# Experts in order of load: four to a step for the twelve lightest, two to a step for the rest

## The chip, the cores and the metric

One core of one Trainium2 chip runs the whole program in one launch. The metric is device time in microseconds (us) of that core. The kernel before takes 1086.76 us, the median of three runs (1086.59 to 1087.28).

## The reference

Two residual layers on 512 tokens of width 1024. Each has a token mixer (layer 0: gated MLP, layer 1: latent attention) with cross-attention beside it, and ends with a mixture of 32 experts: every token picks one of 4 groups and in it the top 2 of 8 experts.

```
combine = sum(one_hot(expert_id, 32) * weights, axis=1)
gate = einsum('td,edf->tef', x, w_gate)      # per expert: 1024 x 256
up   = einsum('td,edf->tef', x, w_up)        # 1024 x 256
act  = silu(gate) * up * combine
y    = einsum('tef,efd->td', act, w_down)    # 256 x 1024
```

All is float32. An expert's three matrices are 3.15 MB, a layer's experts 100.7 MB. 512 tokens with 2 experts each are 1024 places, 32 per expert on average.

## The kernel before, in words

The experts' stage is `moe` (L982). Every expert has 64 slots (`CAP`), so two experts fill the 128 rows of a step, and a layer has 16 steps; step i works on experts 2i and 2i+1. A step gathers its rows from DRAM by token index (`gather`, L989, on the queue of GpSimd), transposes and scales them (`turn`, L998), multiplies by gate and up (`gate_up`, L1008: for each of 8 slices of the inner width one matmul of 512 columns for each of the two experts, each on its own 64 columns of the array), applies silu and the product, transposes (`act_T`, L1024), multiplies by down (`down`, L1033) and adds the rows of the step before into the tokens (`combine`, L1055: 16 matmuls with a 0/1 matrix, split in a high and a low part). TensorE's order is the program order. So is SyncE's, which issues the weight loads, and GpSimd's; VectorE and ScalarE are ordered by the scheduler of the program.

Weights land in a ring of 39 units of 512 KB (`unit`, L76; `NU`, L50). An expert takes six: four with a quarter of gate and up each, two with half the columns of down (`xload`, L244). The rows of every load in DRAM are 2 KB long, and a gate/up unit is filled by two loads of 256 KB. Six experts (`P = NU // 6`, L1569) are loaded before the stage, while the output projection of the mixer runs (`ahead` and `rest`, L1605 and L1609); the other 26 are queued by `nxt` (L1616) after each step, and each load waits on the chip until the unit's old tenant has been read. A load also waits on one of eight semaphores that the loads use in turn.

Ahead of the stage the router gives each token its experts and a slot in each (`choose`, `place`), `count` (L898) finds the fullest expert, and `mark` (L906) and `fill` (L943) build the token lists of four steps at a time with 0/1 matrices of 512 slots. At the end of the program a branch (L1659) runs a slow dense version (`dense_moe`) if any expert had more than 64 tokens. After layer 0 the same ring takes the weights of layer 1's mixer (`soon`, L1638).

Of the kernel before, what the change touches and what calls it, by code (L numbers as in the profile page):

```python
# [9 lines left out]
F32 = mybir.dt.float32  # L10
# [36 lines left out]
class Kern:  # L47
# [194 lines left out]


    def xload(self, layer, e, parts=range(6)):  # L244
        a, eng = self.a, self.nc.sync
        gu = [steps(a[name][layer, e]) for name in ("moe_w_gate", "moe_w_up")]
        d = a["moe_w_down"][layer, e].rearrange("(p j) f -> p j f", j=2)
        tiles = []
        for p in parts:
            w = self.unit([2, 512] if p > 3 else [2, 2, 256], F32, f"x{layer}_{e}")  # L250
            if p > 3:
                eng.dma_start(w, d[:, :, (p - 4) * 512:(p - 4) * 512 + 512])
            else:
                for u in range(2):
                    eng.dma_start(w[:, u], gu[u][:, p // 2, p % 2 * 2:p % 2 * 2 + 2])
            tiles.append(w)
        return tiles

# [472 lines left out]

NE = 32


def moe_constants(K):
# [12 lines left out]

    K.vals = K.const([NT, 2, 8], BF, "vals")
    col = K.const([1], I32, "col")  # L750
    nc.gpsimd.iota(col, pattern=[[0, 1]], base=0, channel_multiplier=1)
    for t in range(NT):
        nc.vector.memset(K.vals[:, t, :, 0:1], float(128 * t - 1024))
        nc.vector.tensor_copy(K.vals[:, t, :, 1:2], col.unsqueeze(1).to_broadcast([128, 2, 1]))
    K.br = [K.const([36], F32, "br") for _ in range(2)]
# [19 lines left out]
class Route:  # L775
# [4 lines left out]
    def __init__(self, K, layer, keep=False):  # L780
        self.K, self.i, self.keep = K, layer, keep
        self.hT, self.lg, self.of, self.o = ([None] * NT for _ in range(4))
        s = lambda shape, name, dt=F32: K.s(shape, dt, tag=name, bufs=1)
        self.r, self.e, self.slot = s([NT], "rr"), s([NT, 2], "re"), s([NT, 2], "rs")
        self.wr = s([NT, 2, 2], "rw")
        self.oh, self.osum = K.t([NT, 2, 32], BF, "oh", 1), K.t([NT, 32], BF, "os", 1)

# [107 lines left out]
        v.scalar_tensor_tensor(out=self.slot[:, S_], in0=self.e[:, S_], scalar=float(CAP), in1=pos, op0=ALU.mult,  # L895
                               op1=ALU.add)

    def count(self):  # L898

        K, nc = self.K, self.K.nc  # L900
        b = K.bank([32])
        for t in range(NT):
            nc.tensor.matmul(b, K.ones, self.osum[:, t], start=t == 0, stop=t == 3)
        nc.vector.reduce_max(K.over[self.i], b, axis=AX.X)

    def mark(self, g, t):  # L906
# [22 lines left out]
    def carry(self, t):  # L929

        K = self.K
        if t == 0:
            self.c0 = K.bank([4, 8])
            self.b0 = [K.bank([512]) for _ in range(2)]
        for n in range(2):
            K.nc.tensor.matmul(self.b0[n], self.of[t], K.x[t][:, n * 512:n * 512 + 512], start=t == 0, stop=t == NT - 1)
        if t == NT - 1:
            self.x0 = K.k4([D], F32, "xg")
            K.nc.vector.tensor_copy(self.x0[:, 0:512], self.b0[0])
            K.nc.scalar.copy(self.x0[:, 512:1024], self.b0[1])  # L940
        self.fill(self.c0, t, self.o[t])

    def fill(self, c, t, o):  # L943

        K = self.K
        for j in range(2):
            for q in range(4):
                K.last_mm = K.nc.tensor.matmul(c[:, q], o[:, j, ts128(q)], K.vals[:, t, j],  # L948
                                               start=(t, j, q) == (0, 0, 0), stop=(t, j) == (3, 1),
                                               skip_group_check=True)  # L950

    def slots(self, c):

        K, nc = self.K, self.K.nc
        v = nc.vector
        tok, wr, idx = K.s([4], tag="tok", bufs=2), K.s([4, 2], tag="wsl", bufs=2), K.s([4], I32, tag="idx", bufs=2)
        iv = K.s([4, 8], tag="iv", bufs=1)
        v.tensor_reduce(tok, c[:, :, 0:2], axis=AX.X, op=ALU.add)
        v.tensor_scalar(idx, tok, 1024.0, 0.0, op0=ALU.add, op1=ALU.max)
        v.tensor_copy(iv, c)  # L960
        v.tensor_add(wr, iv[:, :, 2:4], iv[:, :, 4:6])
        v.tensor_add(wr, wr, iv[:, :, 6:8])
        v.tensor_mul(wr[:, :, 0], wr[:, :, 0], wr[:, :, 1])
        return tok, wr, idx
# [17 lines left out]
def moe(K, layer, R, X, nxt, on_rows, soon):  # L982
# [4 lines left out]
    groups, xg = {0: R.g0}, {0: R.x0}  # L987

    def gather(i):  # L989
        g, c = divmod(i, 4)  # L990
# [7 lines left out]
    def turn(i):  # L998
# [6 lines left out]
                nc.scalar.mul(xT[:, k], b[:, k % 4], K.gain(2 + layer, k))  # L1005
        return xT

    def gate_up(i, xT, between={}):  # L1008
        b = K.bank([2, 256])
        for k in range(8):  # L1010
            if k in between:
                between[k]()
            for h in range(2):
                nc.tensor.matmul(b[h * 64:h * 64 + 64], xT[:, k, h * 64:h * 64 + 64], X[2 * i + h][k // 2][:, :, k % 2],  # L1014
                                 start=k == 0, stop=k == 7, skip_group_check=True)
        s = K.k1([256], F32, "silu")
        g, c = divmod(i, 4)
# [15 lines left out]
    def down(i, aT):  # L1033
        bs = [K.bank([512]) for _ in range(2)]
        for n in range(2):
            for j in range(2):
                for h in range(2):
                    w = X[2 * i + h][4 + n][:, j]
                    nc.tensor.matmul(bs[n][h * 64:h * 64 + 64], aT[:, j, h * 64:h * 64 + 64], w,  # L1039
                                     start=j == 0, stop=j == 1, skip_group_check=True)  # L1040
# [3 lines left out]
        g, c = divmod(i, 4)  # L1044
# [42 lines left out]
    combine(y, range(NT))  # L1087
    y = down(1, aT)
    gather(3)
    for e in range(4):  # L1090
        nxt(e)
    for i in range(2, 16):
        g, part = i // 4 + 1, i % 4
        fills = R.group(g, part) if g < 4 and part < 2 else None
        last = i == 15
        a = gate_up(i, xT, {MID[t]: lambda t=t: combine(y, [t]) for t in range(2)} if last else {})
        if fills is not None:
            fills()
# [6 lines left out]
        else:  # L1105
            combine(old, range(NT))
            aT = act_T(a)
        if i + 1 < 16:
# [4 lines left out]
        if i + 2 < 16:  # L1113
            gather(i + 2)
        for h in range(2):
            if (i, h) == (12, 1):
                soon(0)
            nxt(2 * i + h)
        if i in (12, 14):
            soon(i // 2 - 5)  # L1120
    begin(3, 1)
    combine(y, [0, 1], None, on_rows)
    combine(y, [2, 3], begun, on_rows)
# [381 lines left out]
def dense_moe(K, layer, R, on_rows):  # L1505
# [1 line left out]
    nc, a = K.nc, K.a  # L1507
    v = nc.vector
    cd = K.dram.tile([NE, S], F32, name=K.nm("comb"))
    hT, r = R.hT, [K.s([1], tag=f"dr{t}", bufs=1) for t in range(NT)]  # L1510
    for t in range(NT):
        v.tensor_copy(r[t], R.r[:, t:t + 1])
# [53 lines left out]
def build(tc, ctx, args, out):  # L1566
# [35 lines left out]
    def sparse(layer, phase, on_last, soon=lambda part: None):  # L1602
# [13 lines left out]
        def nxt(e):  # L1616

            e += P
            if e < NE:
                e0 = e - e % 2  # L1620
                for part in range(4) if e == e0 else (4, 5):
                    for z in (e0, e0 + 1):
                        X[z] = X.get(z, []) + K.xload(layer, z, [part])
        moe(K, layer, R, X, nxt, on_last, soon)

    def dense(layer, phase, on_last):
        with manual():
# [65 lines left out]
```

## Time and profile before

| what | value |
|---|---|
| median of 3 runs | 1086.76 us |
| the profiled execution, its own time | 1085.28 us |
| span of the profile | 1083.2 us |
| TensorE busy, share of the span | 97% |
| granted TensorE clock, mean | 0.997 |
| bytes moved | 262.83 MB |

The span begins with the first recorded instruction and ends with the last; the 2.1 us between it and the execution's time lie outside. A busy TensorE in this profile includes matmuls whose ends are modelled. "PEld" is the load of a matmul's stationary operand, "SPq" the instruction queue of SyncE. A DMA share of 1.0 means that all 16 DMA engines have a packet in hand all the time.

### The profile page before, as it was taken

To read this page: it belongs to the slowest core of one execution; us is meant where nothing else is said; L and a number is where in the kernel's file an instruction comes from. 1 tells how busy PE (TensorE), PEld (TensorE's weight loads), DVE (VectorE), ACT (ScalarE), POOL (GpSimd) and SP (SyncE) were. 2 spreads that over 40 slices of the span, in tenths; PEclk is the share of its full clock that TensorE was granted. 3 is DMA by queue.
4 is the path that set the end of the run, shared out by engine and by line. 5 is a ranking of instruction groups with operands and counts; after the bars stand their busy time and mean duration, and the time that the engine had idled before them with its cause. 6 is when DMAs were issued, how large, how long until landed. Compare 5 with 4: busy or idle time off the path is not lost. (4 is left out here: it accounts for less than half of the span.)

```text
span 1083.2 us, 16471 instructions
## 1 busy us (share of the span) xinstructions
PE 1055.4 (97%) x5548; PEld 710.3 (66%) x5548; DVE 576.5 (53%) x1358; ACT 449.9 (42%) x1220; POOL 204.9 (19%) x423
## 2 busy tenths in 40 slices
PE   8999999999999999999999999989999999999996
PEld 6878888886455455444888888868884544554453
DVE  5644686216444455344767677776043544554443
ACT  6846744123321232222747776765032312322230
POOL 3440200014010111110322663410032101111100
PEclk9999999999999999999999999999999999999999
DMA  9432433886999999997022111124968999999972
GB/s 359 129 120 62 136 113 121 301 320 220 373 383 385 380 387 376 386 386 268 25 52 78 50 27 59 59 67 154 377 227 301 384 385 385 380 383 386 379 263 81
DMA packets 135840, 262.83 MB, mean 243 GB/s; under 512 B 14843, under 2 KB 18143, under 8 KB 135748
## 3 DMA queue, kind: packets, MB, share of 16 engines
q1 hardware_dynamic: 129024, 247.12, 63.9%
q0 software_dynamic: 6720, 14.57, 4.0%
q8 instruction: 47, 0.77, 0.3%
q14 instruction: 45, 0.37, 0.1%
q10 hardware_dynamic: 4, 0.00, 0.0%
HBM read 262.17 MB, written 7.34 MB: 249 GB/s over the span
## 5 line engine op out<-in xcount | busy, mean ns | idle before, releaser
L1014 PE MATMUL ps<-x,xT 128*64 128x512 f32 x1024 | 226.9, 593 | 0.1
L1061 DVE TENSOR_TENSOR x<-x,ps 128x512 f32<-128x512 f32 x248 | 153.4, 682 | 120.1 <-PE ps L1053 120.1
L1014 PEld LDWEIGHTS ps<-x,xT 128*64 128x64 f32 x1024 | 75.5, 137 | 140.3 <-issue 137.0
L1039 PE MATMUL ps<-x,actT 128*64 128x512 f32 x512 | 116.8, 598 | 0.0
L1052 PE MATMUL ps<-yh,cm 128*128 128x512 f32 x256 | 103.9, 406 | 0.0
L1053 PE MATMUL ps<-yl,cm 128*128 128x512 f32 x256 | 100.7, 393 | 0.1
L992 POOL MEMSET xg<- 128x1024 f32 x30 | 28.6, 954 | 365.8 <-PE ps L128 321.9
L1019 ACT ACTIVATE silu<-ps,wsl 128x256 f32<-128x256 f32 x32 | 15.2, 476 | 194.9 <-PE ps L1014 194.9
L132 DVE TENSOR_TENSOR yl<-ps,yh 128x512 fp32r<-128x512 f32 x64 | 44.3, 692 | 68.3 <-ACT yh L131 43.0
L116 PE MATMUL ps<-wh,c 128*128 128x512 f32 x192 | 76.5, 398 | 0.0
L118 PE MATMUL ps<-wh,c 128*128 128x512 f32 x192 | 75.0, 390 | 0.0
L117 PE MATMUL ps<-wl,c 128*128 128x512 f32 x192 | 74.8, 389 | 0.0
L1039 PEld LDWEIGHTS ps<-x,actT 128*64 128x64 f32 x512 | 34.1, 136 | 60.7 <-issue 56.1
L1005 ACT ACTIVATE xT<-ps,G 128x128 f32<-128x128 f32 x256 | 69.7, 383 | 6.8 <-PE ps L128 6.5
L1052 PEld LDWEIGHTS ps<-yh,cm 128*128 128x128 f32 x256 | 48.1, 188 | 29.8 <-issue 21.1
L116 PE MATMUL ps<-wh,hh 128*128 128x512 f32 (+1 forms) x160 | 60.9, 381 | 2.2 <-ACT pm L454 1.1
L219 DVE SCALAR_TENSOR_TENSOR wl<-wr,G,wh 128x512 fp32r<-128x512 f32 (+1 forms) x80 | 55.2, 732 | 10.5 <-ACT wh L209 10.2
L131 ACT CAST yh<-ps 128x512 fp32r<-128x512 f32 x64 | 37.5, 586 | 54.3 <-PE ps L1039 53.8
L118 PE MATMUL ps<-wh,hl 128*128 128x512 f32 (+1 forms) x160 | 59.8, 374 | 0.0
L117 PE MATMUL ps<-wl,hh 128*128 128x512 f32 (+1 forms) x160 | 59.8, 373 | 0.0
L144 ACT ACTIVATE junk<-x 128x512 bf16<-128x512 f32 x32 | 20.2, 631 | 90.1 <-DVE x L610 87.4
L1030 ACT COPY actT<-ps 128x256 f32<-128x256 f32 x32 | 11.9, 373 | 107.4 <-PE ps L128 107.4
(350 smaller groups left out, 2041.7 us busy)
## 6 DMA issues: line engine op xcount, KB each, us to landing
x<-in_moe_w_gate_dram SPq DMA_DIRECT2D x256, 256.0 KB
x<-in_moe_w_up_dram SPq DMA_DIRECT2D x256, 256.0 KB
x<-in_moe_w_down_dram SPq DMA_DIRECT2D x128, 512.0 KB
wr<-in_a_w_in_dram SPq DMA_DIRECT2D x20, 512.0 KB
wr<-in_a_w_out_dram SPq DMA_DIRECT2D x12, 512.0 KB
wr<-in_b_w_out_dram SPq DMA_DIRECT2D x12, 512.0 KB
wr<-in_w_mem_kv_dram SPq DMA_DIRECT2D x8, 512.0 KB
wr<-in_b_w_in_dram SPq DMA_DIRECT2D x8, 512.0 KB
```

Of the source, the lines that this page charges most:

```text
L116: mm(out, A[0], B[0], start=first, stop=False)
L117: mm(out, A[0], B[1], start=False, stop=False)
L118: self.last_mm = mm(out, A[1], B[0], start=False, stop=last)
L131: self.gate(self.nc.scalar.copy(hi, src), after)
L132: return self.nc.vector.tensor_sub(lo, src, hi.bitcast(F32))
L219: b = self.nc.vector.scalar_tensor_tensor(out=l, in0=r, scalar=g, in1=h.bitcast(F32), op0=ALU.mult, op1=ALU.subtract)
L1005: nc.scalar.mul(xT[:, k], b[:, k % 4], K.gain(2 + layer, k))
L1014: nc.tensor.matmul(b[h * 64:h * 64 + 64], xT[:, k, h * 64:h * 64 + 64], X[2 * i + h][k // 2][:, :, k % 2], start=k == 0, stop=k == 7, skip ...
L1039: nc.tensor.matmul(bs[n][h * 64:h * 64 + 64], aT[:, j, h * 64:h * 64 + 64], w, start=j == 0, stop=j == 1, skip_group_check=True)
L1052: nc.tensor.matmul(b, cm[:, ts128(t)], yh[:, sl], start=first, stop=False)
L1053: K.last_mm = nc.tensor.matmul(b, cm[:, ts128(t)], yl[:, sl], start=False, stop=last)
L1061: v.tensor_add(K.x[t][:, sl], K.x[t][:, sl], b)
```

## The change

Experts 0 to 5 keep their place: three steps of two, loaded ahead. The other 26 are ranked on the chip by their token count. The 12 with the fewest tokens get 32 slots each and go four to a step (three steps), the other 14 go in pairs of 64 (seven steps): 13 steps in place of 16. `rank` takes the place of `count`; it computes the rank of each expert, the slot shift of its tokens and the list of expert numbers, and the dense branch is also taken when one of the twelve has more than 32 tokens. SyncE reads the expert numbers of a step into registers, two or four, ahead of that step's first load, and the loads take their DRAM address from the register. Each unit now holds one kind of weight, is filled by one load of 512 KB, and its DRAM rows are 4 KB. Because gate and up are in separate units, `gate_up` runs one matmul of 256 columns for gate and one for up. The groups of `mark` and `fill` cover 3, 4, 4 and 2 steps.

```diff
 def xload(self, layer, e, parts=range(6)):
+        gu = [a[name][layer, ds(e, 1)].rearrange("o (a p j) f -> p a (o j) f", a=2, j=4)
+              for name in ("moe_w_gate", "moe_w_up")]
+        d = a["moe_w_down"][layer, ds(e, 1)].rearrange("o (p j) f -> p (o j) f", j=2)
...
+            w = self.unit([1024] if p > 3 else [4, 256], F32, "xw")
+            eng.dma_start(w, d[:, p - 4] if p > 3 else gu[p % 2][:, p // 2])
...
+FIXED, LIGHT = 6, 12
+SORTED = NE - FIXED
+WIDTH = [2] * (FIXED // 2) + [4] * (LIGHT // 4) + [2] * ((SORTED - LIGHT) // 2)
+GROUPS = ((0, 3), (3, 4), (7, 4), (11, STEPS - 11))
...
-    def count(self):
+    def rank(self):
         b = K.bank([32])
         for t in range(NT):
             nc.tensor.matmul(b, K.ones, self.osum[:, t], start=t == 0, stop=t == 3)
-        nc.vector.reduce_max(K.over[self.i], b, axis=AX.X)
+        v.scalar_tensor_tensor(out=key, in0=b[:, FIXED:NE], scalar=float(NE), in1=mine, ...)
+        v.tensor_tensor(out=less, in0=key.unsqueeze(2).to_broadcast([128, n, n]),
+                        in1=key.unsqueeze(1).to_broadcast([128, n, n]), op=ALU.is_gt)
+        v.tensor_reduce(r, less, axis=AX.X, op=ALU.add)
+        v.scalar_tensor_tensor(out=je, in0=r, scalar=K.col, in1=mine, ..., accum_out=e)
+        K.tr(eb, e[0:n])
...
+        v.tensor_copy(self.ids, eb)
...
+    def expert(self, r):
+        return self.K.nc.values_load(self.ids[0:1, r:r + 1], engines=[ENG.SP], min_val=FIXED, max_val=NE - 1)
...
+    def tiles_of(i):
+        w = 128 // WIDTH[i]
+        return [(slice(h * w, h * w + w), {"tile_position": (0, h * w)} if w == 32 else {}) for h in range(WIDTH[i])]
 def gate_up(i, xT, between={}):
-            for h in range(2):
-                nc.tensor.matmul(b[h * 64:h * 64 + 64], xT[:, k, h * 64:h * 64 + 64], X[2 * i + h][k // 2][:, :, k % 2], ...)
+            for u in range(2):
+                for h, (c, tp) in enumerate(tiles_of(i)):
+                    nc.tensor.matmul(b[c, u], xT[:, k, c], X[i][h][k // 4 * 2 + u][:, k % 4], ..., **tp)
 def down(i, aT):
-                for h in range(2):
-                    w = X[2 * i + h][4 + n][:, j]
+                for h, (c, tp) in enumerate(tiles_of(i)):
+                    nc.tensor.matmul(bs[n][c], aT[:, j, c], X[i][h][4 + j][:, n * 512:n * 512 + 512], ..., **tp)
...
-        R.count()
+        R.rank()
+            for i in range(P // 2, STEPS):
+                ids = [R.expert(rank + h) for h in range(WIDTH[i])]
+                for part in range(6):
+                    for h, e in enumerate(ids):
+                        W[i][h] += K.xload(layer, e, [part])
+        def nxt(i):
+            free = 6 * sum(WIDTH[:i + 1])
+            while state["units"] < free and next(stream, stream) is not stream:
+                pass
```

`PhaseC` (the list of layer 1's mixer weights) is made ahead of the last step's down loads, and its first splits come after step 11 (of 0 to 12) instead of step 14 (of 0 to 15): in both one step ahead of the last.

## Rows read from the trace of the kernel before

**Rows 1.** The page: busy time by engine, and the rows by 40 slices of 27.1 us (TensorE's busy tenths, its granted clock, the DMA engines' busy tenths, GB/s).

```profile
PE 1055.4 (97%) x5548; PEld 710.3 (66%) x5548; DVE 576.5 (53%) x1358; ACT 449.9 (42%) x1220; POOL 204.9 (19%) x423
...
PE   8999999999999999999999999989999999999996
...
PEclk9999999999999999999999999999999999999999
DMA  9432433886999999997022111124968999999972
GB/s 359 129 120 62 136 113 121 301 320 220 373 383 385 380 387 376 386 386 268 25 52 78 50 27 59 59 67 154 377 227 301 384 385 385 380 383 386 379 263 81
```

**Rows 2.** TensorE's instructions in order of time (start us, duration us, line): the first matmuls of the experts' stage in layer 1; the last step of layer 0 and of layer 1, from inside gate and up to the first scatter after down.

```profile
822.73 0.69 PE L1014 MATMUL ps<-x,xT 128*64 128x512 f32 x2
...
501.87 1.46 PE L1014 MATMUL ps<-x,xT 128*64 128x512 f32 x6
...
504.38 2.80 PE L1014 MATMUL ps<-x,xT 128*64 128x512 f32 x12
...
509.25 3.65 PE L1039 MATMUL ps<-x,actT 128*64 128x512 f32 x16
512.83 0.50 PE L1052 MATMUL ps<-yh,cm 128*128 128x512 f32 x1
...
1066.50 3.65 PE L1039 MATMUL ps<-x,actT 128*64 128x512 f32 x16
1070.08 0.50 PE L1052 MATMUL ps<-yh,cm 128*128 128x512 f32 x1
```

**Rows 3.** Busy time of each engine in stretches: start:end and length in us, busy us and instructions of PE, PEld, DVE, ACT, POOL, then granted clock, DMA share, GB/s. From 10 to 15 us most bytes come in rows of 4 KB (the input x), in the other stretches in rows of 2 KB.

```profile
10.00:12.50 2.50, 2.32 (x8) 1.69 (x7) 2.50 (x7) 2.50 (x7) 0.00 (x0) 0.72 1.05 411
12.50:15.00 2.50, 2.50 (x8) 1.93 (x8) 1.70 (x3) 2.50 (x7) 1.38 (x3) 0.60 1.02 406
15.00:20.00 5.00, 5.00 (x24) 4.14 (x23) 2.58 (x4) 3.22 (x7) 2.13 (x6) 1.00 1.05 390
205.00:230.00 25.00, 25.00 (x112) 20.69 (x111) 0.93 (x2) 0.73 (x2) 0.00 (x0) 1.00 1.05 387
285.00:480.00 195.00, 195.00 (x1004) 98.52 (x1004) 98.20 (x191) 53.07 (x153) 24.65 (x26) 1.00 1.05 384
842.00:1040.00 198.00, 198.00 (x1018) 99.45 (x1016) 99.15 (x192) 54.57 (x156) 25.50 (x26) 1.00 1.05 383
```

**Rows 4.** SyncE's queue in order of time (start us, us, line): the loads around the start of the stage in layer 0, the last expert loads (down) and the first loads after them.

```profile
259.14 0.33 SPq L255 DMA_DIRECT2D x<-in_moe_w_up_dram  x1
267.44 0.33 SPq L255 DMA_DIRECT2D x<-in_moe_w_gate_dram  x1
...
480.83 2.57 SPq L252 DMA_DIRECT2D x<-in_moe_w_down_dram  x4
483.53 7.25 SPq L189 DMA_DIRECT2D wr<-in_b_w_in_dram  x7
491.58 0.47 SPq L420 DMA_DIRECT2D kT<-kT_d  x1
```

**Rows 5.** The longest waits of SyncE's queue over the whole program (line that waits, what for, us in total, times, longest us).

```profile
SPq L255 <- DMA x<-in_moe_w_down_dram: 112.9, 111, 1.8
...
SPq L255 <- DMA x<-in_moe_w_up_dram: 42.6, 117, 2.7
SPq L255 <- DMA x<-in_moe_w_gate_dram: 38.7, 119, 1.0
...
SPq L255 <- PE ps L1014: 25.0, 29, 8.2
```

**Rows 6.** The DMA queues in 285 to 480 us (packets, MB, share of 16 engines): SyncE's weight loads, and the gathers on GpSimd's queue.

```profile
q1 hardware_dynamic: 38551, 71.48, 99.9%
q0 software_dynamic: 1728, 3.15, 4.4%
```

**Rows 7.** The page's costliest groups, two of TensorE (line, operation, out<-in, rows*columns of the array, size, count | busy us, mean ns of one | idle before).

```profile
L1014 PE MATMUL ps<-x,xT 128*64 128x512 f32 x1024 | 226.9, 593 | 0.1
L1039 PE MATMUL ps<-x,actT 128*64 128x512 f32 x512 | 116.8, 598 | 0.0
```

**Rows 8.** TensorE in order of time: a gate and up of a step on two column halves, two of its operand loads, and four matmuls on all 128 columns.

```profile
341.21 7.04 PE L1014 MATMUL ps<-x,xT 128*64 128x512 f32 x32
...
341.64 0.14 PEld L1014 LDWEIGHTS ps<-x,xT 128*64 128x64 f32 x2 [0.29 <-issue]
342.07 0.14 PEld L1014 LDWEIGHTS ps<-x,xT 128*64 128x64 f32 x2 [0.28 <-issue]
...
819.38 1.98 PE L936 MATMUL ps<-x,of 128*128 128x512 f32 x4 [0.35 <-DVE of L923]
```

**Rows 9.** All engines in order of time at the start of layer 0's stage, where `count` stands.

```profile
264.16 0.25 PE L903 MATMUL ps<-os,ones 128*128 128x32 bf16 x4
...
264.26 1.29 PE L128 MATMUL ps<-ident,xg 128*128 128x128 f32 x8
264.33 0.17 DVE L958 TENSOR_REDUCE tok<-ps 128x4 f32<-128x8 f32 x1 [0.34 <-PE ps L948]
...
264.61 0.18 DVE L904 TENSOR_REDUCE over<-ps 128x1 f32<-128x32 f32 x1
...
265.39 0.16 DVE L963 TENSOR_TENSOR wsl<-wsl 128x4 f32<-128x4 f32 x1
...
265.47 0.69 PE L1014 MATMUL ps<-x,xT 128*64 128x512 f32 x2
```

**Rows 10.** VectorE's groups by size, for the new instructions of `rank` (columns as in rows 7).

```profile
L1061 DVE TENSOR_TENSOR x<-x,ps 128x512 f32<-128x512 f32 x248 | 153.4, 682 | 120.1 <-PE ps L1053 120.1
...
L450 DVE TENSOR_REDUCE s4dt.float<-ps 128x2 f32<-128x512 f32 x16 | 10.8, 682 | 7.3 <-PE ps L118 7.2
...
L1191 DVE TENSOR_TENSOR ra<-ps,tab 128x128 f32<-128x128 f32 (+1 forms) x20 | 5.5, 275 | 5.0 <-ACT qrow L1370 4.8
```

**Rows 11.** SyncE's queue by line (duration ns: min/median/max; first and last start us): reading one value into a register at L1658, with its two checks; the eight stores of the result.

```profile
L1658 SPq TENSOR_LOAD <-ovi x1: 728/728/728, 1041.8 to 1041.8; - x1
L1658 SPq FUSED_REGOPS  x1: 186/186/186, 1042.6 to 1042.6; - x1
L1658 SPq SEQ_ASSERT  x1: 37/37/37, 1042.8 to 1042.8; - x1
...
L1574 SPq DMA_DIRECT2D out_dram<-x x8: 333/392/986, 1072.1 to 1076.7; - x8
```

More of the change, by code (lines that the diff above doesn't have):

```diff
@@ L245, in xload @@
         a, eng = self.a, self.nc.sync
-        gu = [steps(a[name][layer, e]) for name in ("moe_w_gate", "moe_w_up")]
-        d = a["moe_w_down"][layer, e].rearrange("(p j) f -> p j f", j=2)
+        gu = [a[name][layer, ds(e, 1)].rearrange("o (a p j) f -> p a (o j) f", a=2, j=4)
+              for name in ("moe_w_gate", "moe_w_up")]
+        d = a["moe_w_down"][layer, ds(e, 1)].rearrange("o (p j) f -> p (o j) f", j=2)
         tiles = []
         for p in parts:
[L250 to L255, printed above, removed]
+            w = self.unit([1024] if p > 3 else [4, 256], F32, "xw")
+            eng.dma_start(w, d[:, p - 4] if p > 3 else gu[p % 2][:, p // 2])
             tiles.append(w)
@@ L732, with place_of @@
 NE = 32
+FIXED, LIGHT = 6, 12
+SORTED = NE - FIXED
+WIDTH = [2] * (FIXED // 2) + [4] * (LIGHT // 4) + [2] * ((SORTED - LIGHT) // 2)
+STEPS = len(WIDTH)
+GROUPS = ((0, 3), (3, 4), (7, 4), (11, STEPS - 11))
+def place_of(i):
+    return next((g, i - c) for g, (c, n) in enumerate(GROUPS) if i < c + n)
 def moe_constants(K):
@@ L754, in moe_constants @@
         nc.vector.tensor_copy(K.vals[:, t, :, 1:2], col.unsqueeze(1).to_broadcast([128, 2, 1]))
+    K.col = K.const([1], F32, "colf")
+    nc.vector.tensor_copy(K.col, col)
     K.br = [K.const([36], F32, "br") for _ in range(2)]
@@ L896, in place @@
                                op1=ALU.add)
-    def count(self):
+    def rank(self):
         K, nc = self.K, self.K.nc
+        v = nc.vector
+        n = SORTED
         b = K.bank([32])
@@ L903, in count @@
             nc.tensor.matmul(b, K.ones, self.osum[:, t], start=t == 0, stop=t == 3)
-        nc.vector.reduce_max(K.over[self.i], b, axis=AX.X)
+        z = K.k1([8, 32], F32, "rank")
+        key, r, m, d, je = (z[:, i, 0:n] for i in range(5))
+        e, w, move = z[:, 5, 0:1], z[:, 5, 2:4], z[:, 6, 0:2 * NT]
+        less = K.k2([n, n], BF, "less")
+        mine = K.iota16[:, FIXED:NE]
+        v.scalar_tensor_tensor(out=key, in0=b[:, FIXED:NE], scalar=float(NE), in1=mine, op0=ALU.mult, op1=ALU.add)
@@ new lines, in rank @@
+        v.tensor_tensor(out=less, in0=key.unsqueeze(2).to_broadcast([128, n, n]),
+                        in1=key.unsqueeze(1).to_broadcast([128, n, n]), op=ALU.is_gt)
+        v.tensor_reduce(r, less, axis=AX.X, op=ALU.add)
+        v.scalar_tensor_tensor(out=je, in0=r, scalar=K.col, in1=mine, op0=ALU.is_equal, op1=ALU.mult,
+                               accum_out=e)
+        eb = K.bank([n], p=1)
+        K.tr(eb, e[0:n])
+        v.tensor_scalar(m, r, 2.0, -float(LIGHT), op0=ALU.mult, op1=ALU.add)
@@ new lines, in rank @@
+        v.tensor_max(m, m, r)
+        v.scalar_tensor_tensor(out=d, in0=K.iota16[:, 0:n], scalar=-2.0, in1=m, op0=ALU.mult, op1=ALU.add)
+        by = K.k2([2 * NT, n], F32, "by")
+        v.tensor_tensor(out=by, in0=self.oh.rearrange("p t j e -> p (t j) e")[:, :, FIXED:NE],
+                        in1=d.unsqueeze(1).to_broadcast([128, 2 * NT, n]), op=ALU.mult)
+        v.tensor_reduce(move, by, axis=AX.X, op=ALU.add)
+        v.scalar_tensor_tensor(out=flat(self.slot2), in0=move, scalar=CAP / 2.0, in1=flat(self.slot), op0=ALU.mult,
+                               op1=ALU.add)
@@ new lines, in rank @@
+        self.ids = K.s([n], I32, tag="k_ids", bufs=1, p=1)
+        v.tensor_copy(self.ids, eb)
+        v.tensor_scalar(m, r, float(LIGHT), CAP / 2.0, op0=ALU.is_lt, op1=ALU.mult)
+        v.tensor_add(m, m, b[:, FIXED:NE])
+        v.reduce_max(w[:, 0:1], m, axis=AX.X)
+        v.reduce_max(w[:, 1:2], b[:, 0:FIXED], axis=AX.X)
+        v.tensor_max(K.over[self.i], w[:, 0:1], w[:, 1:2])
+    def expert(self, r):
+        return self.K.nc.values_load(self.ids[0:1, r:r + 1], engines=[ENG.SP], min_val=FIXED, max_val=NE - 1)
@@ L946, in fill @@
         for j in range(2):
-            for q in range(4):
+            for q in range(c.shape[1]):
                 K.last_mm = K.nc.tensor.matmul(c[:, q], o[:, j, ts128(q)], K.vals[:, t, j],
@@ L955, in slots @@
         v = nc.vector
-        tok, wr, idx = K.s([4], tag="tok", bufs=2), K.s([4, 2], tag="wsl", bufs=2), K.s([4], I32, tag="idx", bufs=2)
-        iv = K.s([4, 8], tag="iv", bufs=1)
+        n = c.shape[1]
+        tok, wr, idx = (K.s(shape, dt, tag=tag, bufs=2)[:, 0:n]
+                        for shape, dt, tag in (([4], F32, "tok"), ([4, 2], F32, "wsl"), ([4], I32, "idx")))
+        iv = K.s([32], tag="pj", bufs=1).rearrange("p (q v) -> p q v", q=4)[:, 0:n]
         v.tensor_reduce(tok, c[:, :, 0:2], axis=AX.X, op=ALU.add)
@@ L1012, in gate_up @@
                 between[k]()
-            for h in range(2):
-                nc.tensor.matmul(b[h * 64:h * 64 + 64], xT[:, k, h * 64:h * 64 + 64], X[2 * i + h][k // 2][:, :, k % 2],
-                                 start=k == 0, stop=k == 7, skip_group_check=True)
+            for u in range(2):
+                for h, (c, tp) in enumerate(tiles_of(i)):
+                    nc.tensor.matmul(b[c, u], xT[:, k, c], X[i][h][k // 4 * 2 + u][:, k % 4], start=k == 0 and u == 0,
+                                     stop=k == 7, skip_group_check=True, **tp)
         s = K.k1([256], F32, "silu")
-        g, c = divmod(i, 4)
+        g, c = place_of(i)
         wr = groups[g][1][:, c]
@@ L1036, in down @@
             for j in range(2):
-                for h in range(2):
-                    w = X[2 * i + h][4 + n][:, j]
-                    nc.tensor.matmul(bs[n][h * 64:h * 64 + 64], aT[:, j, h * 64:h * 64 + 64], w,
-                                     start=j == 0, stop=j == 1, skip_group_check=True)
+                for h, (c, tp) in enumerate(tiles_of(i)):
+                    nc.tensor.matmul(bs[n][c], aT[:, j, c], X[i][h][4 + j][:, n * 512:n * 512 + 512],
+                                     start=j == 0, stop=j == 1, skip_group_check=True, **tp)
         yh, yl = K.k4([1024], FR, "yh"), K.k4([1024], FR, "yl")
@@ L1089, in moe @@
     gather(3)
[L1090 to L1095, printed above, removed]
+    nxt(1)
+    for i in range(2, STEPS):
+        g, part = next(((g, i - c + 4) for g, (c, n) in enumerate(GROUPS) if g > 1 and 0 <= i - c + 4 < 2), (0, 0))
+        fills = R.group(g, part) if g else None
+        last = i == STEPS - 1
         a = gate_up(i, xT, {MID[t]: lambda t=t: combine(y, [t]) for t in range(2)} if last else {})
@@ L1112, in moe @@
             groups[g] = R.slots(R.c)
-        if i + 2 < 16:
+        if i + 2 < STEPS:
             gather(i + 2)
[L1115 to L1120, printed above, removed]
+        nxt(i)
+        if i == STEPS - 2:
+            soon(2)
     begin(3, 1)
@@ L1509, in dense_moe @@
     cd = K.dram.tile([NE, S], F32, name=K.nm("comb"))
-    hT, r = R.hT, [K.s([1], tag=f"dr{t}", bufs=1) for t in range(NT)]
-    for t in range(NT):
-        v.tensor_copy(r[t], R.r[:, t:t + 1])
+    rd = K.s([NT], tag="dr", bufs=1)
+    hT, r = R.hT, [rd[:, t:t + 1] for t in range(NT)]
+    v.tensor_copy(rd, R.r)
     with K.tc.manual_schedule(engines={ENG.PE}):
@@ L1613, in sparse, with loads @@
         nc.scalar.activation(K.s([1]), R.ex[:, 0:1], AF.Silu)
-        R.count()
[L1616 to L1624, printed above, removed]
+        R.rank()
+        W = {i: [X[2 * i], X[2 * i + 1]] for i in range(P // 2)}
+        state = {"units": 0}
+        def loads():
+            rank = 0
+            for i in range(P // 2, STEPS):
+                ids = [R.expert(rank + h) for h in range(WIDTH[i])]
+                rank += WIDTH[i]
+                W[i] = [[] for _ in ids]
+                for part in range(6):
+                    if (i, part) == (STEPS - 1, 4):
+                        soon(0)
+                    for h, e in enumerate(ids):
+                        W[i][h] += K.xload(layer, e, [part])
+                        state["units"] += 1
+                        yield
+        stream = loads()
+        def nxt(i):
+            free = 6 * sum(WIDTH[:i + 1])
+            while state["units"] < free and next(stream, stream) is not stream:
+                pass
+        moe(K, layer, R, W, nxt, on_last, soon)
     def dense(layer, phase, on_last):
```

17 lines of the change are left out of this document (10 added, 7 removed).

## The prediction

> **What bounds the kernel now.** I read the page first. TensorE is busy in 97% of the span and its granted clock is at full speed; but in the two stretches where the experts run (the 11th to 18th slice and the 32nd to 38th) the DMA engines are also busy all the time, at 373 to 387 GB/s [rows 1]. So the stage has two candidates, and the order of time decides. The first matmul of layer 0's stage starts at 265.47 [rows 9], the last down ends at 509.25 + 3.65 = 512.9 [rows 2]: 247.4 us for 16 steps, 15.46 each. In layer 1 it is 822.73 to 1066.50 + 3.65 = 1070.15, again 247.4. The last expert load has landed by 491.6: the load of kT issued then is the eighth after it, and a load waits for the eighth before it [rows 4]. That is 18 us before down of the last step begins. So TensorE sets the end, with the transfers a step ahead of it. That the transfers are not far behind shows in SyncE's waits: mostly for an earlier load, seldom for TensorE to free a unit [rows 5]. One step's weights, 6.29 MB at 384 GB/s, take 16.4 us, more than the 15.46 of TensorE; the six experts loaded ahead are what keeps TensorE from waiting.
>
> The reader is to keep both budgets in mind: 16 x 15.46 of TensorE, and 26 experts of transfer after a start near 267.4 [rows 4].
>
> **TensorE's side.** Three steps go: 3 x 15.46 = 46.4 us per layer, if a step of four experts takes as long as one of two. The rows speak for it in the case of two: 1024 matmuls of 593 ns, 607 us, fit into 226.9 us [rows 7]; 32 of them take 7.04 us, and four on all 128 columns take 1.98 [rows 8]. So 0.43 us pass per pair on two column halves, as per one on the whole array: both halves run at once. For four quarters no row exists. Between four at once (the price of two) and only two at once (gate and up and down doubled, 7.09 + 3.65 from [rows 7] per step, about 10.5 us more) I take four at once, since the pair loses nothing at all. The matmuls of 256 columns are twice as many for the same columns; two operand loads of 0.14 us leave 0.28 idle per 0.43 [rows 8], so they still fit into half of it, and I cost them at nothing.
>
> `rank` puts a TensorE transpose behind VectorE, ahead of the first step. Where `count` ended with one reduction of 0.18 us [rows 9], the transpose now needs a key (0.18), a comparison of 26 x 26 = 676 elements (676/512 x 0.68 = 0.90), its reduction (0.90) and a selection (0.27) (durations for 512 elements from [rows 10]). That is 2.3 us, and with hand-overs the first step starts some 3.2 later, at 268.7. TensorE alone would then end at 268.7 + 13 x 15.46 = 469.7, against 512.9.
>
> **The transfers' side.** The 26 experts remain: 81.8 MB, plus the gathers (13 in 195 us moved 3.15 MB [rows 6]; the tokens are the same, so about 3.7 MB after the start), 85.5 MB. The rate with 4 KB rows: 411 and 406 GB/s in 10 to 15 us, where such rows dominate, against 384 to 390 with 2 KB rows in four other saturated stretches [rows 3]. I take 409; the ends are 384 (nothing gained) and 411. So 85.5/0.409 = 209 us.
>
> The start moves. Before, the three spare units were loaded by 259.1 and the next load went out at 267.44, as soon as step 0 had freed a unit [rows 4]. Now no load can go before its expert is known. VectorE starts near 264.5 [rows 9], needs the 2.3 us above, the transpose some 0.3 with its hand-over (eight take 1.29 there), then seven small instructions (five of about 0.17, two of 208 elements at some 0.33 by [rows 10]), 1.5 us: 268.6. SyncE then reads four numbers. One read took 0.73, its checks 0.19 and 0.04 [rows 11], with gaps 1.05: 4.2 us. First load near 272.9, 5.5 later, and with three more units (3.8 us) in the stream. If VectorE's scheduler puts the list of numbers earlier or the reads overlap, 3 us less; later, 2 us more.
>
> Before, 84.1 MB from 267.4 at 384 would have ended at 486.4 and had landed by 491.6: 5.2 us for starting up and landing, some of it waits for step 0's units; I take 4. So the last unit lands at 272.9 + 209 + 4 = 485.9. TensorE then cannot start the second half of the last gate and up before the last gate/up unit, four units earlier (4 x 1.28): 480.8. From that half to down were 7.0 us (about 502.3 to 509.25 [rows 2]), then 3.65 of down: 491.4.
>
> So the transfers end 21.7 us later than TensorE could, and set the end: 512.9 - 491.4 = 21.5 us per layer. `rank`'s 3.2 us on TensorE lie beside the stream and cost nothing, unless the array becomes the bound again; then they count in full. TensorE will wait in the wide steps, whose 12.6 MB take 31 us against 15.5, and in the pairs go at the pace of the transfers, 12 x 1.28 + 0.24/0.409 = 16.0 per step against 15.46. The ring holds 39 units, a wide step 24, so 15 are loading while it is computed; units are freed in the order in which they are loaded, and with TensorE waiting for data none of them is late. If the clock drops in those waits as it did at the start (granted 0.72 and 0.60 in 10 to 15, 1.00 after it [rows 3]), half a gate and up takes 7 us instead of 3.5 in the middle of a 31 us step: it fits, but up to 4 us of lag can be left at the first pair, of which 0.5 per step is made up.
>
> SyncE's queue: 156 loads per layer and layer's 26 reads. The reads of a step stand ahead of its loads, so the loads behind them wait 2.1 or 4.2 us; eight loads of 512 KB, 10 us, are in flight by then and cover it. If they are not, each of the nine later steps pays its reads. Layer 1's mixer weights follow the experts on the same queue: seven loads of 1.36 us after 485.9 and the splits on ScalarE, while TensorE needs them at about 491.4 + 7: the first four are there by 491.4. Fewer steps also take their share off VectorE, ScalarE and GpSimd, which set nothing.
>
> **The sum.** 2 x 21.5 = 43 us off the profiled execution's 1085.3 is 1042.3. The runs' median stands 1.5 above that execution: 1044. The case's own bounds: 6.5 less per layer (earlier numbers, 411, a smaller start) is 1031; 6.5 more (later numbers, a lag left over) 1057.
>
> **Rivals.** *Only two quarters at once.* No row excludes it. Three wide steps cost 10.5 us more each; TensorE then ends at 469.7 + 31.5 = 501.2, later than the transfers, and gains 11.7 per layer: 1063. For it: a float32 matmul is two records here, and the second of a quarter must follow the first; against it: the pairs show no such loss. 0.14.
>
> *The rate stays at 384.* Stream 222.7 instead of 209, the end at 504.8, 8.1 per layer: 1070. Against it are 411 and 406 GB/s [rows 3], over 5 us only and beside other traffic, so 0.10. The Trainium skill (DMA: Bandwidth & Descriptors, section Specifications) puts line rate at rows of 512 B and more, and by that rule 4 KB rows would bring nothing; the trace does not agree, as 2 KB rows stand at 384 to 390 and 4 KB rows at 406 to 411 in equally saturated stretches.
>
> *Slower: SyncE becomes the bound.* A load whose address is in a register has no row here. The issues that are shown take 0.33 to 0.99 us [rows 11], and the register arithmetic at least 0.19 more: 0.54 to 1.2 each, under the 1.28 that a unit's transfer takes. With c us per load and 22 more reads (23 us) the stage ends at 512.9 or later from c = 1.34 on. At c = 1.5 it ends at 272.9 + 23 + 234 + 3 + 5.5 = 538, 25.6 later per layer: 1138. For it: the longest issues come near, and they could be longer with a register. Against: the long ones queue behind other transfers. 0.06.
>
> *The dense branch is taken.* The twelfth lightest of the 26 has 28 tokens in both layers and the fullest expert 57, by the reference's routing of its own inputs, so both limits (32 and 64) hold. If it ran, each layer would stream all its experts once more, 2 x 100.7 MB at 384 GB/s or over 500 us in sum. 0.01.
>
> **Numbers.** 0.66 for the forecast, 0.14, 0.10, 0.06 and 0.01 for the rivals, 0.03 for gains and losses that cancel within 0.2%, which is about what a measurement can tell from no change. Faster: 0.66 + 0.14 + 0.10 = 0.90; slower 0.07. The range takes in the forecast's own bounds and the first two rivals, 1030 to 1071, and leaves out the others.
>
> **What would show it.** Right: the DMA engines saturated near 409 GB/s from about 275 to 485; the first load about 273; a wide gate and up as long as a pair's, near 7 us when its data are there; TensorE waiting for weights, some 16 us in the wide steps; down of the last step ending near 491 and the same length from the start in layer 1. Wrong: wide matmuls in two waves (first rival), DMA at 384 (second), SyncE issuing back to back with DMA share well under 1 (third).

## The result, and the profile after

The changed kernel takes 1043.47 us (median of four runs, 1041.96 to 1047.57), the kernel before 1086.67 on the same chip: ratio 0.961 (0.958 to 0.964). The forecast was 1044, with a range of 1030 to 1071. The profiled execution took 1042.26, with a span of 1040.5.

The page of the changed kernel, answering [rows 1, 7]:

```profile
PE 988.2 (95%) x6370; PEld 722.0 (69%) x6370; DVE 540.5 (52%) x1319; ACT 424.1 (41%) x1148; POOL 191.5 (18%) x411
...
PEclk9999999999999899999999999999999999899998
DMA  9432424694799999999222111203964999999993
GB/s 357 150 122 67 142 79 144 246 398 165 259 408 408 408 408 407 406 408 394 70 53 82 52 27 41 80 18 127 369 278 167 389 407 407 408 408 405 408 406 127
...
L1073 PE MATMUL ps<-xw,xT 128*64 128x256 f32 (+1 forms) x2048 | 211.7, 395 | 18.5 <-DMA xw<-in_moe_w_up_dram 16.5
```

Gate and up (now L1073) waited 18.5 us for weights, both layers together; before there was no such wait (0.1). The transfers run at 405 to 408 GB/s in the stage, and TensorE's clock has a dent in each stage. By stretch (columns as in [rows 3]):

```profile
260.00:265.00 5.00, 2.23 (x14) 1.08 (x15) 3.71 (x15) 0.58 (x1) 1.42 (x2) 1.00 0.00 0
265.00:270.00 5.00, 4.97 (x31) 3.50 (x33) 3.97 (x18) 2.17 (x8) 1.76 (x2) 0.66 0.50 123
285.00:470.00 185.00, 175.72 (x1393) 104.72 (x1390) 80.87 (x163) 43.04 (x122) 20.11 (x22) 0.98 1.03 408
810.00:995.00 185.00, 175.82 (x1412) 105.19 (x1410) 79.11 (x161) 45.47 (x131) 19.50 (x20) 0.98 1.03 407
350.00:359.40 9.40, 6.06 (x56) 1.98 (x48) 0.00 (x0) 0.00 (x0) 0.00 (x0) 0.89 1.03 410
359.40:365.00 5.60, 5.53 (x51) 2.50 (x51) 0.00 (x0) 0.00 (x0) 0.00 (x0) 0.58 1.03 407
```

TensorE in order of time, answering [rows 2, 8, 9]: the start, wide steps 3 to 5 (L1097 is down), its last wait for a load in layer 0, the last two downs there, then the count and the last down of layer 1.

```profile
262.17 0.25 PE L918 MATMUL ps<-os,ones 128*128 128x32 bf16 x4
265.03 0.18 PE L128 MATMUL ps<-ident,rank 26*1 26x26 f32 x1 [2.60 <-DVE rank L929]
...
267.05 7.86 PE L1073 MATMUL ps<-xw,xT 128*64 128x256 f32 x64
...
312.18 7.11 PE L1073 MATMUL ps<-xw,xT 128*32 128x256 f32 x128
...
324.65 3.64 PE L1097 MATMUL ps<-xw,actT 128*32 128x512 f32 x32
...
340.58 3.64 PE L1097 MATMUL ps<-xw,actT 128*32 128x512 f32 x32
...
353.07 0.62 PE L1073 MATMUL ps<-xw,xT 128*32 128x256 f32 x2 [0.62 <-DMA xw<-in_moe_w_gate_dram]
...
359.47 5.50 PE L1073 MATMUL ps<-xw,xT 128*32 128x256 f32 x50 [0.22 <-DMA xw<-in_moe_w_up_dram]
...
369.96 3.64 PE L1097 MATMUL ps<-xw,actT 128*32 128x512 f32 x32
...
388.81 3.65 PE L1097 MATMUL ps<-xw,actT 128*64 128x512 f32 x16
...
463.42 3.23 PE L1073 MATMUL ps<-xw,xT 128*64 128x256 f32 x26 [0.43 <-DMA xw<-in_moe_w_up_dram]
...
471.65 3.65 PE L1097 MATMUL ps<-xw,actT 128*64 128x512 f32 x16
...
486.82 3.65 PE L1097 MATMUL ps<-xw,actT 128*64 128x512 f32 x16
...
799.13 0.25 PE L918 MATMUL ps<-os,ones 128*128 128x32 bf16 x4
...
1022.54 3.65 PE L1097 MATMUL ps<-xw,actT 128*64 128x512 f32 x16
```

The count of layer 1 in the kernel before:

```profile
821.41 0.25 PE L903 MATMUL ps<-os,ones 128*128 128x32 bf16 x4
```

From the counting matmuls to the end of the last down there are now 228.3 us in layer 0 (262.17 to 490.47) and 227.1 in layer 1 (799.13 to 1026.19), against 248.7 in both layers before (264.16 to 512.9, 821.41 to 1070.15): 42.1 us less in sum. The spans differ by 42.7: this execution came 2.0 us earlier to its first count (the code up to there is the same), lost 0.1 between the stages, and took 1.3 longer at the end.

SyncE's loads, answering [rows 4], then its reads of expert numbers, answering [rows 11]:

```profile
268.86 2.52 SPq L254 DMA_DIRECT2D xw<-in_moe_w_gate_dram  x4
271.62 3.22 SPq L254 DMA_DIRECT2D xw<-in_moe_w_up_dram  x4
...
470.05 4.18 SPq L254 DMA_DIRECT2D xw<-in_moe_w_down_dram  x4
475.11 8.08 SPq L189 DMA_DIRECT2D wr<-in_b_w_in_dram  x7
484.02 0.41 SPq L419 DMA_DIRECT2D kT<-kT_d  x1
```

```profile
L954 SPq TENSOR_LOAD <-k_ids x8: 262/266/464, 266.1 to 298.0; - x8
L954 SPq FUSED_REGOPS  x8: 147/150/181, 266.6 to 298.3; - x8
```

Four loads take 2.52 us, at most 0.63 each: SyncE with registers is far under the 1.28 us that a unit's transfer takes. The loads of step 3 go out at 268.86, 269.46, 270.18 and 271.1; the fourth needs a unit that step 0 gives back.

### The profile page after: what moved, and what is told of

It reads as the page before. It is cut to its first block, busy times and chain, and to the rows that moved or that the text cites. A ratio compares the mean times of both kernels' runs of the same rounds, so it can differ in the third digit from the quotient of the medians.

```text
span 1040.5 us, 18188 instructions
## 1 busy us (share of the span) xinstructions
PE 988.2 (95%) x6370; PEld 722.0 (69%) x6370; DVE 540.5 (52%) x1319; ACT 424.1 (41%) x1148; POOL 191.5 (18%) x411
## 5 line engine op out<-in xcount | busy, mean ns | idle before, releaser
L1073 PE MATMUL ps<-xw,xT 128*64 128x256 f32 (+1 forms) x2048 | 211.7, 395 | 18.5 <-DMA xw<-in_moe_w_up_dram 16.5
L1073 PEld LDWEIGHTS ps<-xw,xT 128*64 128x64 f32 (+1 forms) x2048 | 121.7, 131 | 112.5 <-DMA xw<-in_moe_w_up_dram 32.1
L1119 DVE TENSOR_TENSOR x<-x,ps 128x512 f32<-128x512 f32 x200 | 123.5, 680 | 122.9 <-PE ps L1111 122.9
L1097 PE MATMUL ps<-xw,actT 128*64 128x512 f32 (+1 forms) x512 | 94.8, 597 | 0.0
L1110 PE MATMUL ps<-yh,cm 128*128 128x512 f32 x208 | 84.7, 407 | 0.0
L1111 PE MATMUL ps<-yl,cm 128*128 128x512 f32 x208 | 81.8, 393 | 0.1
L132 DVE TENSOR_TENSOR yl<-ps,yh 128x512 fp32r<-128x512 f32 x52 | 35.9, 691 | 56.5 <-ACT yh L131 56.5
L1097 PEld LDWEIGHTS ps<-xw,actT 128*64 128x64 f32 (+1 forms) x512 | 27.0, 126 | 49.3 <-issue 37.9
L1059 ACT ACTIVATE xT<-ps,G 128x128 f32<-128x128 f32 x208 | 56.4, 382 | 11.5 <-PE ps L128 11.3
L609 DVE TENSOR_TENSOR x<-x,ps 128x512 f32<-128x512 f32 x16 | 11.0, 687 | 84.6 <-PE ps L118 84.6
L209 ACT ACTIVATE wh<-wr,G 128x512 fp32r<-128x512 f32 (+1 forms) x80 | 51.8, 704 | 1.2 <-DMA wr<-in_w_mem_kv_dram 1.2
## 6 DMA issues: line engine op xcount, KB each, us to landing
xw<-in_moe_w_down_dram SPq DMA_DIRECT2D x128, 512.0 KB, 10.7
```

The source lines that it names most:

```text
L132: return self.nc.vector.tensor_sub(lo, src, hi.bitcast(F32))
L209: a = self.nc.scalar.copy(h, r) if g is None else self.nc.scalar.mul(h, r, g)
L1073: nc.tensor.matmul(b[c, u], xT[:, k, c], X[i][h][k // 4 * 2 + u][:, k % 4], start=k == 0 and u == 0, stop=k == 7, skip_group_check=True, **tp)
L1097: nc.tensor.matmul(bs[n][c], aT[:, j, c], X[i][h][4 + j][:, n * 512:n * 512 + 512], start=j == 0, stop=j == 1, skip_group_check=True, **tp)
L1110: nc.tensor.matmul(b, cm[:, ts128(t)], yh[:, sl], start=first, stop=False)
L1111: K.last_mm = nc.tensor.matmul(b, cm[:, ts128(t)], yl[:, sl], start=False, stop=last)
```

## The experiments

The questions: is it the transfers that end the stage after the change, and what sets their start? The kernel before ran beside each run, at 1086.0 to 1086.2 us; ratios are to it, with a 95% interval.

**The changed kernel once more**, as the measure for the differences of a few us in the runs on the start of the stream. 

> The changed kernel once more, on the chip of the three runs beside it: 1041 to 1047 us by either theory.


1045.95 us, ratio 0.9626 (0.9611 to 0.9642).

**Rows of 2 KB.**

```diff
-... .rearrange("o (a p j) f -> p a (o j) f", a=2, j=4)     # gate, up
+... .rearrange("o (a p j) f -> p a (o j f)", a=4, j=2)
...
-eng.dma_start(w, d[:, p - 4] if p > 3 else gu[p % 2][:, p // 2])
+eng.dma_start(w, d[:, :, p % 2 * 512:p % 2 * 512 + 512] if p > 3 else gu[p % 2][:, p // 2 * 2:p // 2 * 2 + 2])
...                                     # the matmuls address the unit accordingly
```

> The changed kernel with rows of 2 KB in place of 4 KB in all expert loads: the same number of loads, the same bytes, the same register addresses, the same 13 steps. (Gate and up rows then meet other columns of x than they should; the amount of work is the same.) Theory, transfers set the pace of the stage and longer rows are part of the gain: 85.5 MB at the 384 GB/s that the kernel before showed take 222.7 us in place of 209, so about 13.7 us more per layer, about 1070 us (1064 to 1074). Rival, TensorE with its 13 steps is still what ends the stage: no change, 1041 to 1046 us.


1066.40 us, ratio 0.9821 (0.9805 to 0.9837). Its stretches:

```profile
285.00:485.00 200.00, 183.96 (x1428) 108.66 (x1429) 83.16 (x167) 45.12 (x129) 20.08 (x22) 0.97 1.05 386
820.00:1015.00 195.00, 181.75 (x1450) 107.44 (x1448) 77.60 (x160) 43.52 (x126) 17.92 (x19) 0.97 1.04 384
```

The DMA engines are as busy as with 4 KB (1.05 and 1.04 against 1.03), but move 386 and 384 GB/s instead of 408 and 407. From count to last down the stages grew by 11.2 and 10.7 us against the profiled changed kernel; 85.5 MB at 386 instead of 408 are 11.9. The time follows the rate, so the array is not the bound. The size of a load is not what sets the rate: the kernel before moved 384 with gate and up in loads of 256 KB, this run 386 with all loads of 512 KB, both in rows of 2 KB.

**Fewer loads, the same matmuls.**

```diff
 for h, e in enumerate(ids):
+    if h > 1:
+        W[i][h] = W[i][h - 2]
+        continue
...
-free = 6 * sum(WIDTH[:i + 1])
+free = 12 * (i + 1)
```

> The changed kernel, but in a step of four the third and fourth expert use the weight tiles of the first and second: six experts fewer are loaded per layer (18.9 MB), TensorE's work is the same. (Six experts per layer are computed with another expert's weights.) Theory, transfers set the pace: TensorE becomes the bound, 13 steps of 15.46 us from 267.05 end at 468.0 and, with up to 3 us of waits at the start, at 471, against 490.5: 19 to 22 us less per layer, 999 to 1005 us. Rival, TensorE sets the pace because four quarters do not fit in the time of a pair: 1041 to 1046 us.


1001.07 us, ratio 0.9221 (0.9206 to 0.9237): as the theory has it. TensorE's gate and up on the page, then a wide and a paired gate and up with their data there, and the last down of layer 0:

```profile
L1073 PE MATMUL ps<-xw,xT 128*64 128x256 f32 (+1 forms) x2048 | 187.7, 382 | 0.1
```

```profile
346.06 7.09 PE L1073 MATMUL ps<-xw,xT 128*32 128x256 f32 x128
...
361.70 7.13 PE L1073 MATMUL ps<-xw,xT 128*64 128x256 f32 x64
...
467.13 3.65 PE L1097 MATMUL ps<-xw,actT 128*64 128x512 f32 x16
```

The wait of 18.5 us is gone (0.1), and 128 matmuls on quarters take no longer than 64 on halves. The array alone needs 201.9 us in layer 0, from its first gate and up at 268.90 to 470.78: 15.53 per step.

**Other numbers of steps.** Pairs only, and 8 or 16 light experts:

```diff
-FIXED, LIGHT = 6, 12
+FIXED, LIGHT = 6, 0      # and GROUPS ... (11, 4), (15, 1)
+FIXED, LIGHT = 6, 8      # the second kernel
+FIXED, LIGHT = 6, 16     # the third kernel
```

> The changed kernel with no light expert: ranking, register addresses and 4 KB rows as they are, but 16 steps of pairs. Theory: TensorE is the bound again, 16 steps of 15.46 us from 267.05 end at 514.4 in place of 490.5, 24 us more per layer: 1091 us (1088 to 1095), that is 4 to 8 us over the kernel before, which is what ranking costs. Rival, the longer rows or the order by load alone bring the gain: 1043 to 1060 us.


1093.70 us, ratio 1.0067 (1.0046 to 1.0087). TensorE without a gap beside transfers at 406 GB/s:

```profile
285.00:490.00 205.00, 205.00 (x1466) 131.00 (x1464) 101.82 (x207) 55.12 (x157) 25.97 (x28) 1.00 1.03 406
```

Everything of the change but the steps of four loses 7.7 us (5 to 9 by the interval): the array is the bound again and pays for `rank`. In layer 0 it takes 253.4 us from count to last down (261.94 to 515.36), 4.7 more than before. Of these 3.6 are the later first matmul (4.90 behind the count instead of 1.31); 0.7 more is step 0's gate and up, 7.74 instead of some 7.04.

> The changed kernel with 8 light experts in place of 12: two steps of four, 14 steps in all, the same loads. Theory, transfers set the pace: TensorE alone would end at 267.05 + 14 x 15.46 = 483.5, still ahead of the 490.5 at which the stream lets it end, so the time stays, 1042 to 1047 us. Rival, TensorE's number of steps is what the time follows: 15.46 us more per layer, 1074 us.


1043.55 us, ratio 0.9616 (0.9603 to 0.9629).

> The changed kernel with 16 light experts in place of 12: four steps of four, 12 steps in all, the same loads. Theory, transfers set the pace: TensorE alone would end 15.46 us earlier per layer but has to wait for the stream, so the time stays, 1041 to 1046 us. Rival, the number of steps is what the time follows: 15.46 us less per layer, 1012 us.


1045.12 us, ratio 0.9625 (0.9612 to 0.9638).

14, 13 and 12 steps take the same time (ratios 0.9616, 0.9610 to 0.9626 and 0.9625): past two wide steps TensorE only waits more. On the three pages gate and up wait 3.8, 18.5 and 30.8 us.

**What sets the start of the stream.** First the numbers written into the program, then two more experts kept out of the ranking:

```diff
-ids = [R.expert(rank + h) for h in range(WIDTH[i])]
+ids = [FIXED + rank + h for h in range(WIDTH[i])]      # first kernel
...
-FIXED, LIGHT = 6, 12
+FIXED, LIGHT = 8, 12                                   # second kernel
+fixed = i < FIXED // 2
+ids = [2 * i + h if fixed else R.expert(rank + h) for h in range(WIDTH[i])]
+rank += 0 if fixed else WIDTH[i]
```

> The changed kernel with the expert numbers of the loads written into the program (6, 7, 8, ... in order) in place of registers; ranking is still computed. (Experts meet other experts' slots; bytes and steps are the same.) Theory, transfers set the pace and the stream starts late because of the ranking: the three spare units (1.57 MB, 3.9 us at 408 GB/s) are filled before the stage instead of from 268.86 on, so each layer ends about 3.9 us earlier: 1036 us (1033 to 1038). If the register reads and checks between loads cost the stream something too, more than that: under 1033. Rival, the ranking costs because it delays TensorE's first matmul: no change, 1041 to 1046 us.


1038.13 us, ratio 0.9556 (0.9536 to 0.9577): the median is inside its range, 7.8 under the repeat of the changed kernel, but the five runs spread from 1035.42 to 1041.00.

> The changed kernel with experts 6 and 7 kept out of the ranking: they are the pair of step 3 and their loads need no register, so that the stream can fill its three spare units before the ranking is known; 24 experts are ranked, the 12 lightest four to a step, still 13 steps. All is computed. Theory, the stream's late start is what is left to gain at the stage's beginning: three units (3.9 us at 408 GB/s) earlier per layer, 1036 us (1033 to 1038). Rival, the late start is hidden behind TensorE's own late first matmul: no change, 1041 to 1046 us.


1041.56 us, ratio 0.9581 (0.9562 to 0.9599): 4.4 under the repeat. Its interval and the repeat's don't overlap, so there is a gain, but little over half of the theory's; in us it even lies in the rival's range. Its interval overlaps that of the kernel with the numbers written in, so whether these two differ isn't shown. The count and the first gate and up in the second kernel, then SyncE's queue:

```profile
263.36 0.25 PE L918 MATMUL ps<-os,ones 128*128 128x32 bf16 x4
...
267.73 4.58 PE L1073 MATMUL ps<-xw,xT 128*64 128x256 f32 x30
```

```profile
250.48 1.38 SPq L254 DMA_DIRECT2D xw<-in_moe_w_gate_dram  x2
252.98 19.48 SPq L254 DMA_DIRECT2D xw<-in_moe_w_up_dram  x2
```

The three spare units are filled from 250.5 on, but the fourth load goes out at 272.1 (it is the second of its line, 0.33 us long). That is 8.8 us behind the count; in the changed kernel it was 8.9 (262.17 to 271.1). It waits for the first unit that step 0 gives back, half a gate and up after the first matmul (267.73). So the idle time of the transfers was moved behind the three loads and only partly closed. That made another theory: TensorE's first matmul, late by `rank`'s transpose, holds the stream back.

**The transpose behind step 0's gate and up**, with experts 6 and 7 out of the ranking:

```diff
 a = gate_up(0, xT)
+R.rank_ids()     # K.tr(eb, e[0:n]) and the cast to ids, taken out of rank()
 fills()
```

> The kernel with experts 6 and 7 kept out of the ranking, and besides with the transpose that turns the ranked experts' numbers into a row, and the cast behind it, placed behind step 0's gate and up matmuls on TensorE instead of ahead of its first transpose. All is computed. Theory: once the three spare units are filled early, the stream waits for the first tiles that step 0's gate and up matmuls give back, and these start 3.6 us late because TensorE stands before the ranking's transpose; taken away, each layer ends 3 to 4 us earlier, 1041.6 - 7 = about 1035 us (1032 to 1038). Rival, the stream has caught up with that wait anyway by the middle of the stage: 1039 to 1043 us.


1034.09 us, ratio 0.9520 (0.9507 to 0.9533): 7.5 under the kernel with 8 fixed experts, as this theory has it. TensorE, then SyncE's queue:

```profile
262.59 0.25 PE L918 MATMUL ps<-os,ones 128*128 128x32 bf16 x4
262.69 1.34 PE L128 MATMUL ps<-ident,xg 128*128 128x128 f32 x8
263.95 7.13 PE L1077 MATMUL ps<-xw,xT 128*64 128x256 f32 x64
271.01 0.18 PE L128 MATMUL ps<-ident,rank 24*1 24x24 f32 x1
```

```profile
252.76 14.79 SPq L254 DMA_DIRECT2D xw<-in_moe_w_up_dram  x2
267.64 0.86 SPq L254 DMA_DIRECT2D xw<-in_moe_w_gate_dram  x2
```

The first matmul stands 1.36 us behind the count instead of 4.37 (263.36 to 267.73), and the fourth load goes out at 267.2, 4.6 behind the count instead of 8.8. In the two profiled executions, whose spans differ by 8.0 us, the two stages from count to last down are together 5.7 us shorter (224.5 and 221.6 against 226.9 and 224.9); the rest lies ahead of and behind them, where the two kernels do the same. So the trace shows a little less than the 6 to 8 us of the theory.

**Gate before up**, on top of it:

```diff
-for k in range(8):
-    for u in range(2):
+for n, (u, k) in enumerate((u, k) for u in range(2) for k in range(8)):
```

> The same kernel as in the late-transpose run, and in every step the eight gate pieces are multiplied before the eight up pieces instead of alternately. All is computed. Theory: the first two units of step 0 come free after a quarter of the gate and up matmuls instead of after half, about 2 us earlier, so the stream resumes earlier and each layer ends up to 2 us earlier: 1031 to 1035 us. Against it: up's first tile is given back later and wanted no later, so that it comes out even, 1034 to 1038 us.


1033.04 us, ratio 0.9503 (0.9490 to 0.9516). Its fourth load follows the first matmul by 2.0 us instead of 3.3, as meant; but the intervals overlap, so a gain of 1 us isn't shown. In the two profiled executions its stages are together 3.5 us shorter (221.4 and 221.2) and the rest 2.7 longer; one execution of each doesn't decide it.

## Why the prediction was right, and where its steps were not

**The bound.** It said that the transfers would take over from TensorE and end the stage near 491.4. Last down ended at 490.47, in an execution that came 2.0 us earlier to its count; counted from there it is 228.3 us where 227.2 were forecast. Four runs show the cause: slower rows cost what their rate says, fewer bytes gave 20 to 22 us per layer back, and 12 to 14 steps make no difference. Where the transfers bind was not as predicted: TensorE was to wait for the last gate and up unit, at 480.8. The last wait recorded in layer 0 ended at 463.42, a step earlier, and the last step took 15.17 us from down to down (471.65 to 486.82), as long as in the kernel before (15.15), where TensorE set the pace.

**The array.** Four at once was taken, at the price of a pair, 15.46 us per step. Measured were 7.11 us for a gate and up on quarters, and 15.53 per step where no data are late. The first rival (two at once) falls. The Trainium skill (TensorEngine Tiling (Array Packing), Theoretical Speedup) gives up to two times for a dimension of at most 64 and up to four times for one of at most 32; the trace agrees with the step between them, with 128 matmuls on quarters in the time of 64 on halves.

**The rate.** 409 GB/s was taken, 405 to 408 measured; the second rival (384) falls. (The prediction's 384 to 390 for 2 KB rows is 383 to 390 in its rows.) The Trainium skill (DMA: Bandwidth & Descriptors, Specifications) gives about 358 GB/s from HBM for each core, as half of a stack's 716, and line rate from transfers of 512 B on. The runs, with one core at work, differ from both: 386 GB/s with 2 KB rows and 408 with 4 KB rows, the bytes, loads and steps alike.

**SyncE.** Loads with a register went out 0.6 us apart, under half of the 1.34 from which the third rival decides. The dense branch was not taken.

**The start: the weakest step.** The first load was predicted at 272.9 and found at 268.86. Of the 4.0 us, 2.0 are the earlier execution; most of the rest are the four reads, which took 2.5 us (266.1 to 268.6) instead of 4.2. Yet the stage ended only 0.9 us earlier than predicted, because three later terms were too small. The transfers took 0.6 us longer at 408 GB/s. The 4 us for starting up and landing were 5.6: the eighth load after the last expert's went out at 484.02, and 85.5 MB at 408 GB/s from 268.86 end at 478.4. From there, the last landing, to the end of down it took 6.5 us instead of 5.5, since TensorE was the later of the two in the last step. The errors had opposite signs; that the end came out closer than its terms is luck.

"`rank`'s 3.2 us on TensorE lie beside the stream and cost nothing" doesn't hold as a rule. The delay was 3.6 us (4.88 behind the count, before 1.31), and it holds back the units that step 0 returns. The first load and the first returned unit bound the stream together: taking the loads off the ranking gave 4.4 us, taking TensorE off it too gave 11.9, both for two layers. What the delay costs in the changed kernel, whose first loads are themselves late, no run separates; there the fourth load followed the third by 0.9 us, where the second followed the first by 0.6.

**The waits.** Some 16 us were predicted in the wide steps. From down to down, step 5 took 29.4 us (340.58 to 369.96), 13.9 over a step; the first pair took 18.8. As feared, the clock gave way: TensorE worked 6.06 of 9.4 us and was then granted 0.58 for 5.6 us, near its lower level of 1.2 GHz. It costs nothing in that place, since the transfers run on at 407 GB/s. The page's 18.5 us of waits don't hold all that TensorE lost. Gate and up were also busy 24.0 us longer than in the run with fewer loads (211.7 against 187.7), part of it at the lower clock. Both together are 21.3 us per layer; layer 0's stage took 223.4 us from its first gate and up (267.05 to 490.47) against 201.9 there, 21.5 more.

## What to carry to other kernels

When a change lifts one bound, count the next one in bytes and rate. Here two wide steps would have been enough; what the runs gained or lost beyond them came from the bytes, the rate and the start of the stream. A producer that fills a ring of buffers can't go past the spare ones before the consumer gives back its first. A delay of the consumer's first instruction is then paid by the producer too, even if the consumer waits for data later. Work that decides later addresses goes behind the first step that doesn't need it, with enough fixed work ahead to cover it. The two versions built so are the fastest here that load every expert's weights, at 1034.09 and 1033.04 us.

## What the runs showed of the hardware that was not expected

- Of the eight reads into a register on SyncE above, the first took 0.46 us and the seven after it 0.26 to 0.27, with 0.15 to 0.18 for the arithmetic of each one's check; the single read of before took 0.73 [rows 11].
- A pause at the stage's start can cost TensorE clock. After `rank` (2.23 us busy in 260 to 265, above) it was granted 0.66 in 265 to 270, and step 0's gate and up took 7.86 us; in the run with the late transpose, without the pause, 1.00 and 7.13. It isn't so each time: in layer 1 of the changed kernel's execution gate and up took 7.13 right behind a pause of the same 2.60 us. What decides it is open.
- A VectorE instruction of `rank` on 26 values took 0.97 us while GpSimd cleared a tile (MEMSET) for the next gather, one of the same form 0.17 a little later. It stands ahead of the cast to the list of numbers (at 265.90), for which SyncE's reads wait. Other runs show the same pair (0.97 beside 0.97); none moves the clearing away, so the cause and what it costs are open. In the changed kernel:

```profile
264.76 0.97 POOL L1046 MEMSET xg<- 128x1024 f32 x1
264.80 0.97 DVE L934 TENSOR_SCALAR rank<-rank 128x26 f32<-128x26 f32 x1
...
266.55 0.17 DVE L946 TENSOR_SCALAR rank<-rank 128x26 f32<-128x26 f32 x1
```

- Executions differ by some 2 us before the stage, where the code is the same. In the twelve traces the count of layer 0 begins between 261.94 and 264.16: at 261.94 to 263.36 where the first 50 us were granted 1.00, at 263.78 to 264.16 where 0.97. The cause wasn't looked for.
